# Projecting Q ahead of K, taking the recurrence's rows later, and summing three modulation pieces in place on DVE

## The chip, the cores and the metric

The kernel runs on one core of a Trainium2 chip. The time is that of one execution on the device, in microseconds (us); smaller is better. The kernel before took 792.27 us, the median of three runs (791.53 to 793.74).

The engines are named as in the profile: PE is TensorE's matmul, PEld its weight load, DVE is VectorE, ACT is ScalarE, POOL is GpSimd, and SP is SyncE, which here does nothing but issue loads and stores. Each engine works through its own instructions in the order in which the program lists them; an instruction waits for the others by semaphores.

## The reference

Two layers over 256 latent tokens and 256 context tokens of width 1024, all in float32. Cut to what matters:

```python
for layer in range(2):
    mod = silu(c) @ ada_w[layer] + ada_b[layer]            # 6 * 1024 values: shift, scale, gate, twice
    shift1, scale1, gate1, shift2, scale2, gate2 = split(mod, 6)
    h = rmsnorm(x, norm_mix[layer]) * (1 + scale1) + shift1
    if layer == 0:
        q, k, v, xb, gb = split(h @ w_in, ...)             # also k, v, xb of the context tokens
        attn = neighbourhood_attention(norm(q), norm(k), v, ...)   # 8 heads, context keys in the same softmax
        y = bidirectional_rglru(conv(xb), ...)             # gates, then a scan in each direction
        mix = concat(attn, gelu(gb) * y) @ w_out
    else:
        mix = real(fft2(h by groups of channels)) @ fnet_w
    x = x + gate1 * mix
    h2 = rmsnorm(x, norm_ffn[layer]) * (1 + scale2) + shift2
    x = x + gate2 * grouped_moe(h2)                        # router, top 2 of 16 experts, silu(h g) * (h u) @ d
```

`mod` is a product of one vector with a 1024 x 6144 matrix in each layer. The kernel cuts that matrix into 12 pieces of 512 columns for each layer, named (layer, j). Pieces (1, 7), (1, 8) and (1, 9), which the change is about, hold the second half of layer 1's second shift and all of its second scale but no gate; they are first used when layer 1's expert stage begins.

## The kernel before

**Weights.** All large weights stream through 16 buffers ("slots") of 128 x 2048 float32, 1 MiB each. `Stream` holds a list of items in a fixed order. SP issues the next item's load as soon as a slot is free, and never an item ahead of its turn; a slot is free once the last instruction that reads it is done. A modulation piece is two slots (four of the eight 128-row blocks in each), a projection of 512 columns is two, an expert is two for each of its gate (`g`), up (`u`) and down (`d`) matrices. The order in the front is written out in `ORDER`: "a" is the next modulation piece of the list `ADA`, Q, G and V are projections, B the attention bias, o and p the halves of the output projection. Then come four more pieces of layer 0 and two of layer 1 (`FILL0`), the experts of layer 0 in pairs (g, u, d, each four slots), layer 1's mixing weights `fw`, the three pieces of `GAP` and two more (`FILL1`), and the experts of layer 1.

**A modulation piece on PE** (`ada_te`, L324): 32 products in four column tiles, the columns of a piece against the silu of the conditioning vector; ACT copies the result out of PSUM (`gvr`, L337), PE transposes it (L339), and DVE adds the bias into `modc` (L350). `ada_step` does this in two steps for the projections' loops: the products in the first, the transposes in the second. `side(n)` runs n such steps.

**Projections.** A weight block is split into a high part (ACT, L371) and a remainder (L372, on POOL or DVE), and three matmuls replace one (`mm3`, L384 to L386). `gemm` (L580) runs the eight blocks of a projection and splits two blocks ahead; the strings `EK`, `EQ`, `EG`, `EV` choose the engine of each remainder, "g" for POOL and "v" for DVE. Before the projections of this section, xb has been projected.

**The order of layer 0's mixing.** PE's order is written by hand (`manual_schedule`); the order on the other engines is made by a planner, which goes by the program's order as a priority and by when it holds an instruction to be ready. PE's order before: K's eight blocks, each followed by `conv(2)` (the convolution, DVE), by a modulation step and from block 3 on by the first direction's gates (`gates[0]`, strings `W_K`); then Q with the steps of the first direction's recurrence (`scan[0]`, string `W_Q`); then the gate branch G with the rest of `scan[0]` and the head norm's transposes (`hk`); then V with `hq`, `gates[1]` and `scan[1]`. Each `head_norm` has one step of arithmetic (ACT squares, DVE sums and scales) and then one step with transposes for each 128 tokens. Both directions' gates live in two buffers R and I, which the pool holds once: the second direction's are written when the first direction's scan is through. In `scan`, ACT makes the exponential, tanh and square root, DVE the sums and products and the scan itself, POOL the products with I.

Then a loop of 20 steps (L849) runs attention: unit u is a head and half of the queries. A step computes scores for two units (PE), the softmax of the unit before (DVE bias, DVE maximum, ACT exponential, DVE scaling) and the transposes of earlier ones. Beside it, steps 0 to 5 run a modulation step each, steps 0 to 3 run `cat_rec` (the recurrence's rows times the gate on POOL, split on ACT and POOL), and steps 4 to 17 run one step each of the output projection (`project`), two more coming after the loop.

**Experts** (`moe`, L875; `up`, L1034; `down`, L1066): a pair's gate and up products, `act` on DVE, PE transposes, the down products, then ACT and DVE make `yH` and `yL`, which `scatter` adds into the result. The first pairs come right after the router; pair p's weights are items (g, u, d) of p.

**Between the layers** (L1193 on): `normed` adds the experts' result and normalizes (DVE, ACT). Meanwhile PE has, ahead of the DFT in its order, the products of the three `GAP` pieces (`ada_pe`, L1195), whose transposes come after the normalized input (`issue_after`). Then the DFT (L1211 on), the projection with `fw`, and layer 1's experts.

## Time and profile before

| | before |
|---|---|
| median of three runs | 792.27 us (791.53 to 793.74) |
| the profiled execution | 794.38 us, of which the profile's span is 792.6 |
| mean granted clock of TensorE in it | 0.957 |
| PE busy | 708.8 us (89% of the span) |
| DVE, ACT, POOL busy | 277.2, 241.6, 129.6 us |
| loaded and stored | 277.41 MB, mean 350 GB/s |

The profile is of one execution. Its times count from the first instruction. PE's busy time includes time in which matmuls overlap in the pipeline, so 89% does not mean that PE is at its limit for that share. Averages over the span say little here, since the stages have different limits; the sections below go by stage. "Granted clock" is the share of full speed at which TensorE was clocked, at one of two levels (1.2 and 2.4 GHz), averaged over a stretch.

### The profile page before, as it was taken

The numbers are of one execution on the slowest core, as the hardware profiler recorded it, in microseconds if no ns is written. First come the engines' busy times: TensorE is split into PE (matmuls) and PEld (weight loads), VectorE is DVE, ScalarE is ACT, GpSimd is POOL, SyncE is SP. The second block draws the span as 40 slices with busy tenths as digits, with TensorE's granted clock in tenths as the row PEclk, the third lists the DMA queues.
The fourth block names the chain that finished last, engine by engine and source line by source line (L and its number), as shares of the span: only waits on it lengthen the run. The fifth ranks groups of instructions, "written<-read, shape, count | busy, mean of one in ns | idle before, by whom it ended". The sixth has DMA issues, their size and how long they took to land. (4 is left out here: it accounts for less than half of the span.)

```text
span 792.6 us, 11546 instructions
## 1 busy us (share of the span) xinstructions
PE 708.8 (89%) x4707; PEld 388.6 (49%) x4707; DVE 277.2 (35%) x551; ACT 241.6 (30%) x432; POOL 129.6 (16%) x109
## 2 busy tenths in 40 slices
PE   3999979994997799799999997899699799999996
PEld 2677659563775633343444333667434343344334
DVE  3556388166654511111121104344511111121115
ACT  6233955963665310100110003254310110111001
POOL 1243271363321200000000001032201000000002
PEclk8899998996999899999999999899799999999998
DMA  8989756485656789999999999999299999999995
GB/s 275 356 329 385 311 222 264 167 304 228 265 196 253 296 358 421 416 405 421 421 420 423 418 421 422 420 420 351 112 374 422 417 411 421 421 420 420 423 399 170
DMA packets 53793, 277.41 MB, mean 350 GB/s; under 512 B 4898, under 2 KB 20832, under 8 KB 22496
## 3 DMA queue, kind: packets, MB, share of 16 engines
q1 hardware_dynamic: 53008, 275.95, 87.0%
q8 instruction: 41, 0.67, 0.3%
q10 hardware_dynamic: 720, 0.59, 0.2%
q14 instruction: 24, 0.20, 0.1%
HBM read 275.47 MB, written 1.05 MB: 349 GB/s over the span
## 5 line engine op out<-in xcount | busy, mean ns | idle before, releaser
L1042 PE MATMUL g<-slot,xg 128*64 128x512 f32 x512 | 116.2, 608 | 7.9 <-PEq L1145 7.9
L1079 PE MATMUL dn<-slot,aT 128*64 128x512 f32 (+1 forms) x544 | 114.1, 571 | 3.2 <-DVE aT L1063 3.2
L1042 PE MATMUL u<-slot,xg 128*64 128x512 f32 x512 | 113.0, 592 | 0.0
L372 POOL TENSOR_TENSOR wp<-slot,wp 128x512 fp32r<-128x512 f32 x50 | 68.8, 1385 | 161.6 <-ACT wp L371 161.5
L1042 PEld LDWEIGHTS g<-slot,xg 128*64 128x64 f32 x512 | 38.3, 140 | 81.7 <-issue 80.8
L1048 DVE TENSOR_TENSOR act<-act,u 128x512 f32<-128x512 f32 x16 | 11.0, 687 | 192.1 <-PE u L1042 192.1
L1042 PEld LDWEIGHTS u<-slot,xg 128*64 128x64 f32 x512 | 38.0, 137 | 72.2 <-issue 71.7
L1079 PEld LDWEIGHTS dn<-slot,aT 128*64 128x64 f32 x544 | 37.5, 137 | 68.5 <-issue 60.2
L331 PE MATMUL gv<-slot,sc 128*32 128x128 f32 x1536 | 58.2, 293 | 12.1 <-DMA slot<-in_ada_w_dram 7.7
L1081 ACT ACTIVATE yH<-dn,gcol 128x512 fp32r<-128x512 f32 (+1 forms) x34 | 22.5, 662 | 130.5 <-PE dn L1079 125.3
L997 ACT ACTIVATE xg<-xg,modc,a 128x256 f32<-128x256 f32 x32 | 18.0, 564 | 136.5 <-PE xg L988 136.5
L331 PEld LDWEIGHTS gv<-slot,sc 128*32 128x32 f32 x1536 | 47.8, 118 | 24.0 <-issue 13.0
L999 POOL TENSOR_TENSOR SG<-S,gates 128x512 f32<-128x512 f32 x8 | 8.4, 1044 | 310.5 <-PE st L1051 302.1
L1082 DVE SCALAR_TENSOR_TENSOR yL<-dn,gcol,yH 128x512 fp32r<-128x512 f32 (+1 forms) x34 | 24.4, 719 | 93.6 <-ACT yH L1081 85.4
L371 ACT ACTIVATE wp<-slot 128x512 fp32r<-128x512 f32 x72 | 44.3, 627 | 38.0 <-PE qp L386 11.6
L1047 ACT ACTIVATE act<-g 128x512 f32<-128x512 f32 x16 | 9.6, 597 | 121.4 <-PE g L1042 121.4
L988 PE MATMUL xg<-S,xh 128*128 128x256 f32 x128 | 28.4, 306 | 3.8 <-DVE S L976 2.6
L995 DVE TENSOR_SCALAR xg<-xg,a,modc 128x256 f32<-128x256 f32 x32 | 17.4, 543 | 29.4 <-ACT xg L997 29.4
L988 PE MATMUL xg<-S,xl 128*128 128x256 f32 x128 | 27.4, 298 | 0.0
L1019 PE MATMUL ya<-yH,ST 128*128 128x512 f32 x60 | 26.2, 437 | 0.5 <-ACT yH L1081 0.2
L988 PEld LDWEIGHTS xg<-S,xh 128*128 128x128 f32 x128 | 22.1, 209 | 5.5 <-issue 3.2
L1019 PE MATMUL ya<-yL,ST 128*128 128x512 f32 x60 | 23.9, 399 | 0.9 <-DVE yL L1082 0.9
(252 smaller groups left out, 1047.0 us busy)
## 6 DMA issues: line engine op xcount, KB each, us to landing
slot<-in_moe_g_dram SPq DMA_DIRECT2D x64, 1024.0 KB, 13.5
slot<-in_moe_u_dram SPq DMA_DIRECT2D x64, 1024.0 KB, 15.2
slot<-in_moe_d_dram SPq DMA_DIRECT2D x60, 1024.0 KB, 16.3
slot<-in_ada_w_dram SPq DMA_DIRECT2D x40, 1024.0 KB, 8.3
slot<-in_w_in_dram SPq DMA_DIRECT2D x8, 1024.0 KB, 7.2
slot<-in_ada_w_dram SPq DMA_DIRECT2D x12, 512.0 KB, 9.0
slot<-in_w_out_dram SPq DMA_DIRECT2D x4, 1024.0 KB, 6.3
slot<-in_fnet_w_dram SPq DMA_DIRECT2D x4, 1024.0 KB, 19.8
```

What stands on the lines that cost most here:

```text
L331: te.matmul(out=p[32 * q:32 * q + 32, 0:128], lhsT=sc32[:, k, :], rhs=W[:, k, c:c + 128], start=(k == 0), stop=(k == 7))
L371: ac.activation(dst_h, src, AF.Copy)
L372: eng.tensor_tensor(dst_l, src, dst_h.bitcast(F32), op=ALU.subtract)
L988: at_xg[0] = te.matmul(out=p[:, i * 256:(i + 1) * 256], lhsT=xx[:, tb, k * 128:(k + 1) * 128], rhs=S[:, tb * 256:(tb + 1) * 256], start=(n ...
L995: ve.tensor_scalar(xg[:, k], pv, a2[:, k:k + 1], b2[:, k:k + 1], op0=ALU.mult, op1=ALU.add)
L997: ac.activation(xg[:, k], pv, AF.Identity, scale=a2[:, k:k + 1], bias=b2[:, k:k + 1])
L1019: te.matmul(out=yacc[tb * 2 + h], lhsT=ST[:, tb * 128:(tb + 1) * 128], rhs=y[:, h * 512:(h + 1) * 512], start=(p == 0 and n == 0), stop=(n ...
L1042: te.matmul(out=q[half(i), :], lhsT=xg[:, k, half(i0 + i)], rhs=W[i][:, k], start=(k == 0), stop=(k == 7))
L1048: ve.tensor_tensor(act, act, gu[1], op=ALU.mult)
L1079: te.matmul(out=dn[half(i), :], lhsT=aT[:, fc * 128 + 64 * i:fc * 128 + 64 * i + 64], rhs=W[i][:, fc, c], start=(fc == 0), stop=(fc == 3))
L1081: ac.activation(yH[:, c], dn, AF.Copy, scale=gcol)
L1082: ve.scalar_tensor_tensor(yL[:, c], dn, gcol, yH[:, c].bitcast(F32), op0=ALU.mult, op1=ALU.subtract)
```

## The change

- In the front, Q's projection comes ahead of K's. `conv`, one channel block a step, and five of the modulation steps go beside Q; the first direction's gates and the first steps of its recurrence beside K; the rest of that recurrence and the arithmetic of Q's head norm beside G, where K's transposes come one a step after block 3; Q's transposes go to V's first blocks. The stream's order (`ORDER`) follows. The strings that give each remainder's engine change: all of Q's on POOL, three of K's eight on DVE; G's and V's stay.
- One modulation piece less is done ahead of V, so the loop of attention runs other pieces, and (1, 6) comes after the loop (`side(99)`).
- In the loop, `cat_rec` runs in steps 2 to 5 rather than 0 to 3, and the output projection in steps 6 to 19 rather than 4 to 17.
- Pieces (1, 7), (1, 8), (1, 9) are loaded after the down weights of layer 0's pairs 4, 5 and 6 rather than after `fw`. The new `ada_inplace` multiplies and adds a piece's eight blocks into its first one on DVE (8 instructions of 128 x 512) after the pair's down products; one pair later, after `up`, PE sums over the partitions with four products against a column of ones, and DVE adds the bias. The products in PE's order between the layers go.

```diff
--- before.py
+++ after.py
@@ -31,20 +31,21 @@
 
 FILL0 = [[(0, 10), (0, 11)], [(1, 4), (1, 5)], []]
 FILL1 = [[(1, 10), (1, 11)], [], []]
-GAP = [(1, j) for j in (7, 8, 9)]
-
-ORDER = 'aaaQaBaaGaaVaapoa'
-
-EK = 'ggggvggg'
-EQ = 'vgvgvgvg'
+
+BESIDE = [(1, j) for j in (7, 8, 9)]
+
+ORDER = 'aaKaaBaGaaVaaapoa'
+
+EK = 'gvggvggv'
+EQ = 'gggggggg'
 EG = 'vgvgvgvg'
 EV = 'ggvggvgg'
 EO = 'ggvggvggvggvggvg'
 EF = 'vvggggvggvvggvgg'
 
-W_K = ('11111111', '00022220')
-W_Q = ('00010000', '11311111')
-W_G = ('00010000', '12221100', '00001111')
+W_Q = '11101010'
+W_K = ('00100010', '22220000', '00001222')
+W_G = ('00010000', '22221000')
 W_V = ('01001010', '00001321', '22220000')
 
 
@@ -229,6 +230,8 @@
                 r += [(c, a // 512, slice(a % 512, a % 512 + b - a)) for a, b in zip(CUTS, CUTS[1:]) for c in pair]
             else:
                 r += [(c, i) for i in range(2) for c in pair]
+            if l == 0 and n == "d" and p - 4 in range(len(BESIDE)):
+                r.append(ada_item(*BESIDE[p - 4]))
         return r
 
     WQ, WK, WV, WXB, WGB = range(5)
@@ -280,7 +283,7 @@
         load_ada(ks)
         load_wx(ks[0])
 
-    st.add([win_item(WK)])
+    st.add([win_item(WQ)])
     st.pump()
 
     cols = const.tile([128, 190], F32, name="cols")
@@ -364,6 +367,23 @@
         second = ada_te(l, [(W, q * 128, 4 * j + q) for q in range(4)], ps_=wps, used=W.used, late=True)
         yield
         second()()
+        yield
+
+    def ada_inplace(l, j):
+
+        W = st.get(("a", l, j))
+        r = W[:, 0]
+        ve.tensor_scalar(r, r, sc32[:, 0, 0:1], None, op0=ALU.mult)
+        for k in range(1, 8):
+            ve.scalar_tensor_tensor(r, W[:, k], sc32[:, k, 0:1], r, op0=ALU.mult, op1=ALU.add)
+        W.done(1)
+        yield
+        p = wps("gv")
+        for q in range(4):
+            te.matmul(out=p[:, q:q + 1], lhsT=r[:, q * 128:(q + 1) * 128], rhs=ones[:, 0:1], start=True, stop=True)
+        c4 = slice(4 * j, 4 * j + 4)
+        ve.tensor_tensor(modc[l][:, c4], p[:, 0:4], ada_b[l][:, c4], op=ALU.add)
+        W.done(0)
         yield
 
     def split(dst_h, src, dst_l, eng):
@@ -534,7 +554,7 @@
     gw = [t[:, 1536:2048].rearrange("p (d b j) -> p d b j", d=2, b=4) for t in bg]
     for g in range(2):
         nc.sync.dma_start(out=gw[g], in_=gate_w[:, g])
-    named = {"Q": [win_item(WQ)], "G": [win_item(WGB)], "V": [win_item(WV)],
+    named = {"K": [win_item(WK)], "G": [win_item(WGB)], "V": [win_item(WV)],
              "B": [(bias_t[i], na_bias[:, 4 * i:4 * i + 4]) for i in range(2)],
              "o": [st.chunk(("wo", 1), w_out[1])], "p": [st.chunk(("wo", 0), w_out[0])]}
     ada = iter(ADA)
@@ -544,7 +564,7 @@
     st.add([ada_item(*a) for n in FILL0 for a in n])
     st.add(exp_items(0))
     st.add([st.chunk(("fw", h), fnet_w[h]) for h in range(2)])
-    st.add([ada_item(*a) for a in GAP + [a for n in FILL1 for a in n]])
+    st.add([ada_item(*a) for n in FILL1 for a in n])
     st.add(exp_items(1))
     for c in (a_s[1], a_s[3], Wx):
         for i in range(2):
@@ -677,47 +697,49 @@
 
     by_hand = ExitStack()
     by_hand.enter_context(tc.manual_schedule(engines={mybir.EngineType.PE}))
-    kp = [acc("kp") for _ in range(4)]
     conv = Task(convolution())
     rec = [Recurrence(d) for d in range(2)]
     gates = [Task(r.gates()) for r in rec]
     scan = [Task(r.scan()) for r in rec]
     side = Task(*[ada_step(*a) for a in ADA])
-    for n, _ in enumerate(gemm(st.get(("win", WK)), lambda w, k: rows(kp, w, 4, k), EK)):
-        conv(2)
-        side(int(W_K[0][n]))
-        if n == 3:
-            softplus()
-        gates[0](int(W_K[1][n]))
-    evacuate(kp, kr)
-    gates[0](99)
-    side(1)
     qp = [acc("qp") for _ in range(2)]
     for n, _ in enumerate(gemm(st.get(("win", WQ)), lambda w, k: rows(qp, w, 2, k), EQ)):
-        scan[0](int(W_Q[1][n]))
-        side(int(W_Q[0][n]))
+        conv(1)
+        side(int(W_Q[n]))
+        if n == 5:
+            softplus()
+    conv(99)
     qr = [t2k("qr")[:, 0:512] for _ in range(2)]
     evacuate(qp, qr)
+    side(1)
+    kp = [acc("kp") for _ in range(4)]
+    for n, _ in enumerate(gemm(st.get(("win", WK)), lambda w, k: rows(kp, w, 4, k), EK)):
+        gates[0](int(W_K[1][n]))
+        scan[0](int(W_K[2][n]))
+        side(int(W_K[0][n]))
+    evacuate(kp, kr)
     hk, hq = Task(head_norm(kr, kT, kn)), Task(head_norm(qr, qT, qn8))
     hk(1)
-    hq(1)
     side(1)
     gb2 = [acc("gbp") for _ in range(2)]
     gbp = [gb2[b // 2][:, (b % 2) * 256:(b % 2) * 256 + 256] for b in range(4)]
     for n, _ in enumerate(gemm(st.get(("win", WGB)), lambda w, k: channels(gbp, w, 256, k), EG)):
         scan[0](int(W_G[1][n]))
         side(int(W_G[0][n]))
-        hk(int(W_G[2][n]))
+        if n == 1:
+            hq(1)
+        if n > 3:
+            hk(1)
     scan[0](99)
+    hk(99)
     evacuate(gb2, [gTf[:, 0:512], gTf[:, 512:1024]])
-    hk(99)
     side(1)
 
     vp = [acc("vp") for _ in range(4)]
     for n, _ in enumerate(gemm(st.get(("win", WV)), lambda w, k: rows(vp, w, 4, k), EV)):
         side(int(W_V[0][n]))
-        if n == 0:
-            hq(99)
+        if n < 2:
+            hq(1)
         gates[1](int(W_V[2][n]))
         scan[1](int(W_V[1][n]))
         if n == 6:
@@ -725,6 +747,7 @@
         if n % 4 == 3:
             st.give(s_h[n // 4])
             st.give(s_h[2 + n // 4])
+    hq(99)
     scan[1](99)
     v = a8("v", [128, 4, 512])
     for t in range(4):
@@ -850,9 +873,9 @@
         att()
         if u < 6:
             side(1)
-        if u < 4:
+        if 2 <= u < 6:
             cat()
-        elif u < 18:
+        if u >= 6:
             mp = next(mix)
     side(99)
     att(99)
@@ -1099,6 +1122,8 @@
                     gate = gate_rows(l, 40)
                     overflow(l, ci, over, xh, xl, a2, b2, gate)
                 u = up(p, xg)
+                if l == 0 and p - 5 in range(len(BESIDE)):
+                    next(beside)
                 if p == 0:
                     for f in fins:
                         f()
@@ -1118,6 +1143,9 @@
                 if p == 5 and l == 0:
                     load_dft()
                 pend = down(u[0], act_t, *u[2:])
+                if l == 0 and p - 4 in range(len(BESIDE)):
+                    beside = ada_inplace(*BESIDE[p - 4])
+                    next(beside)
                 if p % 2 == 1 and p < 7:
                     xg = xg_
             if store:
@@ -1192,13 +1220,9 @@
     dts = []
     xn, _ = normed(mp, gate)
     yacc, gate = moe(0, xn, False)
-    fins = [ada_pe(*a, ps_=(gps, wps, wps)[i]) for i, a in enumerate(GAP)]
 
 
     xn, last = normed(yacc, gate, a8("xn", [128, 2, D]))
-    with tc.issue_after(last.ins):
-        for f in fins:
-            f()
     dt = dts[0]
     a1 = scale_col("a1_1", modc[1], 8, g_mix[1])
     b16 = const.tile([128, 8], F32, name="b16")
```

## Rows read from the trace of the kernel before

**Rows 1.** Stages: us, busy PE, PEld, DVE, ACT, POOL (x), clock, DMA, GB/s.
```profile
103.00:123.00 20.00, 14.84 (x61) 10.65 (x65) 19.09 (x22) 7.67 (x15) 11.21 (x8) 0.83 0.54 211
123.00:140.00 17.00, 17.00 (x238) 16.43 (x230) 12.43 (x20) 11.23 (x22) 4.48 (x4) 1.00 0.67 249
...
175.00:190.00 15.00, 4.11 (x76) 3.11 (x77) 11.56 (x20) 5.10 (x12) 8.17 (x10) 0.70 0.72 281
...
276.00:490.00 214.00, 204.69 (x977) 83.70 (x974) 37.22 (x65) 25.41 (x41) 6.92 (x5) 0.99 0.99 411
490.00:572.00 82.00, 63.32 (x558) 47.49 (x558) 40.50 (x92) 34.73 (x74) 18.72 (x13) 0.90 0.84 342
```

**Rows 2.** What SP's load queue waited for: us in total, times, longest us.
```profile
SPq L128 <- PE g L1042: 104.5, 22, 24.3
```

**Rows 3.** SP in order of time, 455 to 500: start, length, count.
```profile
456.04 8.04 SPq L128 DMA_DIRECT2D slot<-in_moe_d_dram  x4
...
476.21 22.68 SPq L128 DMA_DIRECT2D slot<-in_ada_w_dram  x10
```

**Rows 4.** The loads of 455 to 464.5, issue to landing.
```profile
DMA to landing us min/median/max: 20.1/20.1/20.1
```

**Rows 5.** PE in order of time, 380 to 585: start, us, [idle before <-releaser].
```profile
480.44 7.09 PE L1079 MATMUL dn<-slot,aT 128*64 128x512 f32 x32
...
496.15 1.94 PE L331 MATMUL gv<-slot,sc 128*32 128x128 f32 x32 [5.61 <-DMA slot<-in_ada_w_dram]
...
507.12 2.68 PE L1211 MATMUL f<-dft,xn 128*128 128x257 f32 x10
...
509.73 1.08 PE L331 MATMUL gv<-slot,sc 128*32 128x128 f32 x32
```

**Rows 6.** Groups by line, 276 to 490: count, busy us, mean ns.
```profile
L1082 DVE SCALAR_TENSOR_TENSOR yL<-dn,gcol,yH 128x512 fp32r<-128x512 f32 x16 | 12.0, 751 | 51.5 <-ACT yH L1081 47.4 <-issue 4.1
```

**Rows 7.** PE in order of time, 108 to 125, in Q.
```profile
111.76 0.51 PE L385 MATMUL qp<-wp,h 128*128 128x512 f32 x1 [0.89 <-POOL wp L372]
...
117.55 0.79 PE L385 MATMUL qp<-wp,h 128*128 128x512 f32 x1 [4.12 <-DVE wp L372]
...
118.14 0.63 PE L386 MATMUL qp<-wp,h 128*128 128x512 f32 x1
...
122.53 2.13 PE L331 MATMUL gv<-slot,sc 128*32 128x128 f32 x64
```

**Rows 8.** DVE in order of time, three stretches.
```profile
69.39 4.42 DVE L577 SCALAR_TENSOR_TENSOR xcT<-xb,cols,xcT 128x512 f32<-128x512 f32 x5
...
184.24 1.27 DVE L762 TENSOR_REDUCE mx<-s 128x1 f32<-128x512 f32 x2
...
498.91 0.75 DVE L417 TENSOR_SCALAR xn<-xt,rs 128x1024 f32<-128x1024 f32 x1
```

**Rows 9.** The table of stages, 496 to 503.
```profile
496.00:503.00 7.00, 5.60 (x97) 4.11 (x97) 2.85 (x6) 1.72 (x4) 0.00 (x0) 0.58 1.01 418
```

**Rows 10.** ACT in order of time, two stretches.
```profile
146.79 1.26 ACT L641 ACTIVATE R<-gp,cols 128x512 f32<-128x512 f32 x2
...
186.31 0.42 ACT L371 ACTIVATE catH<-yl 128x256 fp32r<-128x256 f32 x1 [1.63 <-POOL yl L737]
...
188.04 0.69 ACT L765 ACTIVATE P<-s,mx 128x512 f32<-128x512 f32 x1
```

**Rows 11.** PE in order of time, two stretches around attention.
```profile
189.04 0.47 PE L339 MATMUL gv<-cst,gvr 128*128 128x128 f32 x1 [10.19 <-ACT gvr L337]
...
198.77 1.50 PE L331 MATMUL gv<-slot,sc 128*32 128x128 f32 x46 [0.69 <-ACT PT L781]
...
242.65 0.41 PE L331 MATMUL gv<-slot,sc 128*32 128x128 f32 x2 [0.93 <-DVE catL L372]
```

**Rows 12.** POOL in order of time, 60 to 80.
```profile
70.59 2.67 POOL L372 TENSOR_TENSOR wp<-slot,wp 128x512 fp32r<-128x512 f32 x1 [5.84 <-ACT wp L371]
...
78.35 1.27 POOL L372 TENSOR_TENSOR wp<-slot,wp 128x512 fp32r<-128x512 f32 x1 [3.40 <-ACT wp L371]
```

## The prediction

> **What bounds the kernel now.** I read the table of stages first, then the load queue, then TensorE around each place that the diff touches.
>
> The stages [rows 1] show two kinds of time. In layer 0's expert stage (276 to 490 us) the DMA share is 0.99 at 411 GB/s, so the load stream sets the pace. Ahead of it, from 103 to 190 us, the DMA share is 0.54 to 0.72 and PE has holes. In the bridge between the two expert stages (490 to 572) DMA falls to 0.84.
>
> The load queue shows what ties the stages together. It waits for PE's gate products to free a buffer for 104.5 us in all, 24.3 at the longest [rows 2]: this is the bridge's end, with all 16 buffers full. So layer 1's experts always start with the same stock, and the end of the kernel is their start plus a constant. That start is layer 0's start, plus its expert stage, plus the bridge. I cost each of the three.
>
> Is layer 0's expert stage bound by PE or by DMA? By both at once. Its last four loads are issued from 456.04 to 464.08 [rows 3] and land 20.1 us after issue [rows 4], so the last at about 483.8. The last down product starts at 480.44 and takes 7.09 [rows 5]; its second half, which needs that load, starts at 484.0. There is no slack.
>
> **Part 1, three pieces move into the expert loads: +14.9.** Each piece is two buffers, so six more stand in the queue ahead of layer 0's last down weights. Ten such loads were issued in 22.68 us under a full queue [rows 3], (22.68 - 0.33)/9 = 2.48 us each. Six are 14.9, and with no slack the end of the stage moves by all of it. If PE's clock falls while it waits for loads, the last half-product (3.5 us) could take twice as long: bounds 14.9 to 18.4.
>
> The summing on DVE is 24 instructions of 128x512, bounded by yL's 0.75 us [rows 6]: at most 18 us. They hide, since DVE is busy for 37 of the 214 us [rows 1]. The added wait is for the piece's load; behind it on DVE stand the next pair's products, for which PE's transposes wait. But weights queued after a piece land after it, so PE stands for those anyway; without that cover one piece is up to 6 us. The 12 one-column products on PE, between zero and the 0.63 us of a slow 512-column one [rows 7] (7.6 in all), lie in PE's waits too.
>
> **Part 2, the bridge without those pieces: -5.7.** Now PE has the three pieces' products ahead of the DFT in its order and waits for their loads, at first 5.61 us [rows 5]. The normalized input is there at 498.91 + 0.75 = 499.7 [rows 8], the DFT starts at 507.12, and 1.08 us of a piece still lies inside it [rows 5]. Without them it can start 7.5 earlier and run 1.1 shorter: -8.6. What is late next is that input, off DVE. But PE then does nothing from 490 to 499.7, and the DFT meets the lower clock. After the shorter idle time of now, 496 to 503 has a granted clock of 0.58 [rows 9], so 7 us x 0.42 = 2.9 are lost. Bounds: nothing, and twice that, as the idle time is nearly twice as long. I take 2.9, the row of the same place.
>
> **Part 3, the front: -5.0.** Removed: the Q projection stops twice, 0.89 and 4.12 us, for weight splits, the longer time on DVE; then 11 matmuls from 117.55 to 122.53 run at the lower clock (0.63 us each) [rows 7], which loses half of 5 us. Together 7.5. The recurrence's arithmetic fills DVE at that time: 19.09 of 20 us busy [rows 1]. In the new order it comes with K's end and with G. One piece (two halves of 1.08 [rows 5], 2.1 us) also leaves the part ahead of V. If nothing came in their place, V would start 9.6 earlier.
>
> What comes in their place? The recurrence now meets K's head norm on DVE, beside G, and four of G's eight splits are on DVE. The two windows from 103 to 140 hold 31.5 us of DVE work [rows 1], which the new order packs from K's last steps into G, so DVE is as full as in the stretch that stalled. The return is between 0 and 7.5; I take 3.75, half: the arithmetic is the same, but K's steps, twice Q's in length, can take some of it. Separately, V's gates need the buffers that the first direction holds until DVE is done: 31.5 us from about 105 end at about 137, against a need at 146.79 [rows 10] less 9.6. That just fits. So V gains 5.85, and with it the second direction's scan.
>
> Attention starts late now: PE stands 10.19 us until 189.04 [rows 11], behind ACT, which writes the last output row at 186.31 and loads a table before the first exponential at 188.04 [rows 10]. The first of the two row maxima that end at 184.24 + 1.27 [rows 8] is there at 184.9. With those output rows two units later, the exponential could come 3.1 earlier. But ACT's order is a planner's, and these rows already run there ahead of exponentials that the program issues first; so 0 to 3.1, and I take 1.5.
>
> The piece that left the front comes back after attention: 2.1, plus up to 0.47 for its transposes, less the wait of 0.93 that it covers [rows 11]: +1.6. The output projection moves from units 4 and 5 to 18 and 19, so these two have less to hide the softmax. Such a unit waits 0.69 now [rows 11]: 0 to 1.4, I take 0.7. The front is -5.85 - 1.5 + 1.6 + 0.7 = -5.0.
>
> The loads that change places in the front cost nothing as long as PE's freeing of buffers sets their times; the idle DMA there [rows 1] is the cover. Without it, one load is 2.5.
>
> One more effect can touch Q. POOL now makes all eight split remainders while DVE runs the convolution; a split takes 1.27 us on POOL by itself and up to 2.67 [rows 12] beside that convolution (69.39 to 73.81 [rows 8]). Q's work on PE is 48 matmuls of 0.23 (half of the slow 0.45 in [rows 7]) and three pieces: 17.3 us. The Trainium skill ("SBUF — State Buffer", Who interferes with whom) says that a DVE instruction with two SBUF inputs and a GpSimd one that reads SBUF exclude each other for a whole instruction, and that speaks against this edit. The trace agrees with it in those two rows. By the rows alone: eight at 2.67 are 21.4, so 4.1 lost; with half at 1.27 they are 15.8, and nothing is lost. The convolution ends at 74, ahead of the last splits, so I count nothing here and keep 4.1 as a rival.
>
> **Sum.** +14.9 - 5.7 - 5.0 = +4.2 us. The profiled execution took 794.38, its span 792.6 and 1.8 around it; with the sum it is 798.6. It lies 2.1 over the median of 792.27, so the forecast is 796.5, 0.5% slower. A measurement can tell about 0.3% (2.4 us) from no change.
>
> **Rivals.**
> - *DVE keeps up in G* (the other side: not slower). Place: DVE between K's last steps and V. It decides whether splits and norms come in time, with the first direction's last scan before V's gates need its buffers. For it: K's longer steps. Against: the full DVE [rows 1]. Price: V gains 9.6, attention 3.1, no extra softmax wait: front -9.6 - 3.1 + 1.6 = -11.1, total -1.9, 790.4.
> - *The same, and the DFT meets the full clock*: a further -2.9, 787.5.
> - *The whole stop returns in G, and ACT's order stays*: front -2.1 + 1.6 + 0.7 = +0.2, total +9.4, 801.7. For it: the same instructions on the same engines.
> - *POOL is late in Q*: 796.5 + 4.1 = 800.6.
> - *The added loads cost nothing*, because the stream has room I don't see: 796.5 - 14.9 = 781.6. Against: [rows 1, 3].
> - *The later rows change nothing*, as ACT's order stays: 798.0, inside the forecast's own range of 793.5 to 799.5.
>
> **How the numbers follow.** Forecast 0.44 (0.34 of it slower by over 2.4 us, 0.10 within), DVE keeps up 0.24 (0.16 within, 0.08 faster), the full clock too 0.10 (faster), the stop returns 0.12, POOL late 0.05, loads free 0.05. Faster 0.08 + 0.10 + 0.05 = 0.23; within 0.10 + 0.16 = 0.26; slower 0.34 + 0.12 + 0.05 = 0.51. The range runs from 787.5, the full-clock case, to 801.7, the returning stop, and leaves out the free loads and half of each outer case's spread.
>
> **What would show it.** Part 1: PE waits for gate, up and down loads in the last three pairs of layer 0, some 15 us in all; no such waits, and it falls. Part 2: DFT within 1 us of the normalized input, clock near 0.6 at first. Part 3: no stop over 1 us in Q; in G, matmuls that wait for DVE's splits or for head norm; PE's stop at attention's start shorter than 10. I am wrong if the first expert stage grows by less than 12, or if V starts over 8 us earlier.

## The result and the profile after

| | before | after |
|---|---|---|
| median of the runs beside each other | 793.0 us | 800.24 us |
| profiled execution, its span | 794.38, 792.6 | 800.24, 798.2 |
| mean granted clock | 0.957 | 0.964 |

The ratio is 1.0084, with a 95% interval from 1.0066 to 1.0102: slower by 7.2 us, where 4.2 was forecast. The trace shows 5.6 of it (the spans). In stages, each worked out from the first or last start or end of the matmuls named, in us from the start:

| stretch | before | after | change | forecast |
|---|---|---|---|---|
| first projection matmul to layer 0's first gate matmul | 61.94 to 275.28: 213.3 | 61.47 to 275.09: 213.6 | +0.3 | -5.0 |
| layer 0's experts, to the end of the last down product | 487.52: 212.2 | 502.51: 227.4 | +15.2 | +14.9 |
| bridge, to layer 1's first gate matmul | 571.65: 84.1 | 577.63: 75.1 | -9.0 | -5.7 |
| layer 1's experts, to PE's last matmul | 215.3 | 215.4 | +0.1 | 0 |

(The first projection matmul itself came 0.5 earlier, and what follows PE's last matmul is 0.5 shorter.) So the largest term came as forecast, the front gave nothing of its 5.0, the bridge gave 3.3 more, and two errors partly cancel.

**Layer 0's experts.** After, PE's timeline from 440 to 503 (start, us, operation; in brackets the idle time before and what ended it) shows what [rows 5] did not have, waits for gate and up loads:

```profile
447.54 3.65 PE L1065 MATMUL u<-slot,xg 128*64 128x512 f32 x16 [0.77 <-DMA slot<-in_moe_u_dram]
452.51 3.65 PE L1065 MATMUL u<-slot,xg 128*64 128x512 f32 x14 [1.32 <-DMA slot<-in_moe_u_dram]
...
470.87 1.97 PE L1065 MATMUL g<-slot,xg 128*64 128x512 f32 x2 [4.04 <-DMA slot<-in_moe_g_dram]
473.35 8.64 PE L1065 MATMUL g<-slot,xg 128*64 128x512 f32 x29 [0.51 <-DMA slot<-in_moe_g_dram]
483.29 3.65 PE L1065 MATMUL u<-slot,xg 128*64 128x512 f32 x16 [0.86 <-DMA slot<-in_moe_u_dram]
488.27 3.65 PE L1065 MATMUL u<-slot,xg 128*64 128x512 f32 x14 [1.33 <-DMA slot<-in_moe_u_dram]
```

The waits named are 8.8 us of the 15.2. The rest lies inside groups that PE stretches while their weights arrive, such as the 8.64. On DVE, one piece's sums are 8 instructions, 0.49 + 2.32 + 3.11 = 5.9 us, and one of them waits:

```profile
465.66 0.49 DVE L376 TENSOR_SCALAR slot<-slot,sc 128x512 f32<-128x512 f32 x1 [0.67 <-DMA slot<-in_ada_w_dram]
468.29 2.32 DVE L378 SCALAR_TENSOR_TENSOR slot<-slot,sc 128x512 f32<-128x512 f32 x3
470.64 3.11 DVE L378 SCALAR_TENSOR_TENSOR slot<-slot,sc,slot 128x512 f32<-128x512 f32 x4
```

**The bridge.** The normalized input is there 12.1 us after the last down product in both kernels (before: [rows 5, 8]). After, on PE and on DVE:

```profile
511.70 9.26 PE L1235 MATMUL f<-dft,xn 128*128 128x257 f32 x32 [6.18 <-DVE xn L437]
520.81 0.59 PE L1252 MATMUL pq<-Y,dft 128*128 128x254 f32 x2
```
```profile
510.82 0.74 DVE L437 TENSOR_SCALAR xn<-xt,rs 128x1024 f32<-128x1024 f32 x1
...
513.90 0.75 DVE L437 TENSOR_SCALAR xn<-xt,rs 128x1024 f32<-128x1024 f32 x1
```

and the table of stages (us, busy time and count of PE, PEld, DVE, ACT, POOL, then clock, DMA share, GB/s):

```profile
511.70:514.60 2.90, 2.90 (x6) 1.82 (x6) 1.92 (x4) 1.45 (x3) 0.00 (x0) 0.50 1.01 415
514.70:520.80 6.10, 6.09 (x26) 5.06 (x27) 3.38 (x14) 2.47 (x7) 0.00 (x0) 0.98 1.01 422
```

The DFT does meet the lower clock: 0.50 of full speed, the level of 1.2 GHz. But it begins with the first 128 tokens, whose half of the input is there at 511.56, and only six of its 32 matmuls run on that half alone. They have nothing to hurry for: the second half comes at 514.65, and the seventh starts at 514.71. From there on the clock is 0.98.

**The front.** PE in G, after:

```profile
116.01 0.39 PE L406 MATMUL gbp<-h,wp 128*128 128x256 f32 x1 [1.74 <-DVE wp L392]
119.93 0.38 PE L406 MATMUL gbp<-h,wp 128*128 128x256 f32 x1 [0.80 <-DVE wp L392]
128.77 0.65 PE L637 MATMUL ht<-cst,kq 128*128 128x128 f32 x4 [4.44 <-DVE kq L631]
137.06 1.95 PE L334 MATMUL gv<-slot,sc 128*32 128x128 f32 x64 [0.53 <-DVE modc L353]
```
```profile
128.77:133.00 4.23, 4.23 (x23) 4.23 (x24) 4.23 (x4) 1.32 (x2) 2.89 (x3) 0.60 0.71 250
```

Q has no stop any more (PE is busy for 19.00 of the 19 us from 61 to 80), and G has 1.74 + 0.80 + 4.44 + 0.53 = 7.5 us of them, all for DVE, which is busy for 26.96 of the 27 us from 112 to 139. Behind the longest of them the clock is 0.60 for 4.2 us (the second block: stretch, busy times, clock), which loses 1.7 more: 9.2 in all, where Q lost 5.0 by stops and 2.5 by the clock [rows 7]. At attention's start, first DVE, then ACT, then PE:

```profile
183.18 1.27 DVE L785 TENSOR_REDUCE mx<-s 128x1 f32<-128x512 f32 x2
```
```profile
185.26 0.42 ACT L391 ACTIVATE catH<-yl 128x256 fp32r<-128x256 f32 x1 [1.63 <-POOL yl L760]
185.69 1.28 ACT L788 ACT_TABLE_LOAD   x1
186.99 0.69 ACT L788 ACTIVATE P<-s,mx 128x512 f32<-128x512 f32 x1
...
187.66 0.27 ACT L340 ACTIVATE gvr<-gv 128x128 f32<-128x128 f32 x1
```
```profile
187.98 0.47 PE L342 MATMUL gv<-cst,gvr 128*128 128x128 f32 x1 [11.10 <-ACT gvr L340]
```

The four output rows (catH) still stand ahead of the first exponential (P), though the program now issues them later; PE's stop is 11.10, against 10.19 [rows 11].

The +0.3 of the whole front is in part luck. Up to the end of the output projection it is 1.2 longer (187.3 against 186.1, from the first projection matmul). The stretch behind that, the same code in both, gives 0.9 back, and there the clock differs. Here are its last matmuls, which gather the experts' tokens, before and after:

```profile
269.82:275.25 5.43, 5.43 (x32) 5.33 (x32) 1.30 (x3) 1.69 (x3) 0.97 (x1) 0.69 0.85 353
```
```profile
271.11:275.20 4.09, 4.09 (x34) 3.96 (x36) 1.45 (x3) 1.70 (x3) 0.97 (x1) 1.00 1.01 427
```

### The profile page after: what moved, and what is told of

Its sections match the earlier page's. It is cut to its first block, busy times and chain, and to the rows that moved or that the text cites. A ratio compares the mean times of both kernels' runs of the same rounds, so it can differ in the third digit from the quotient of the medians.

```text
span 798.2 us, 11217 instructions
## 1 busy us (share of the span) xinstructions
PE 708.3 (89%) x4536; PEld 385.6 (48%) x4536; DVE 295.5 (37%) x573; ACT 245.3 (31%) x432; POOL 133.8 (17%) x111
## 5 line engine op out<-in xcount | busy, mean ns | idle before, releaser
L1065 PE MATMUL g<-slot,xg 128*64 128x512 f32 x512 | 119.4, 611 | 13.6 <-PEq L1173 7.8
L1065 PE MATMUL u<-slot,xg 128*64 128x512 f32 x512 | 115.6, 593 | 4.3 <-DMA slot<-in_moe_u_dram 4.3
L392 POOL TENSOR_TENSOR wp<-slot,wp 128x512 fp32r<-128x512 f32 x52 | 73.6, 1422 | 152.2 <-ACT wp L391 152.1
L334 PE MATMUL gv<-slot,sc 128*32 128x128 f32 x1344 | 50.4, 288 | 3.8 <-ACT sc L307 2.0
L334 PEld LDWEIGHTS gv<-slot,sc 128*32 128x32 f32 x1344 | 41.2, 115 | 14.1 <-issue 7.2
L392 DVE TENSOR_TENSOR wp<-slot,wp 128x512 fp32r<-128x512 f32 x20 | 17.9, 898 | 19.7 <-ACT wp L391 19.7
## 6 DMA issues: line engine op xcount, KB each, us to landing
slot<-in_moe_d_dram SPq DMA_DIRECT2D x60, 1024.0 KB, 16.2
slot<-in_w_in_dram SPq DMA_DIRECT2D x8, 1024.0 KB, 12.1
```

Source lines behind the costliest of these rows:

```text
L334: te.matmul(out=p[32 * q:32 * q + 32, 0:128], lhsT=sc32[:, k, :], rhs=W[:, k, c:c + 128], start=(k == 0), stop=(k == 7))
L392: eng.tensor_tensor(dst_l, src, dst_h.bitcast(F32), op=ALU.subtract)
L1065: te.matmul(out=q[half(i), :], lhsT=xg[:, k, half(i0 + i)], rhs=W[i][:, k], start=(k == 0), stop=(k == 7))
```

## The experiments

A short table first; the sections behind it say what each is. V start, row maximum (end of attention's first two) and first P transposes count from the first projection matmul; all of them and the three stages are worked out from each kernel's trace, the ratio from its runs.

| kernel | median us | ratio, 95% interval | V start | row max. | P transposes | first gate matmul | layer 0 | bridge |
|---|---|---|---|---|---|---|---|---|
| before | 793.0 | | 78.0 | 123.6 | 133.1 | 213.3 | 212.2 | 84.1 |
| after | 800.2 | 1.0084 [1.0066, 1.0102] | 77.5 | 123.0 | 132.8 | 213.6 | 227.4 | 75.1 |
| e2_beside | 800.2 | 1.0076 [1.0052, 1.0100] | 78.3 | 123.9 | 133.6 | 213.8 | 227.7 | 75.5 |
| e5_pe_beside | 799.0 | 1.0069 [1.0052, 1.0086] | 77.0 | 122.6 | 132.1 | 212.4 | 227.2 | 75.4 |
| e3_swap | 784.0 | 0.9886 [0.9856, 0.9915] | 77.1 | 122.6 | 132.1 | 212.4 | 212.1 | 74.4 |
| e4_without | 783.4 | 0.9873 [0.9853, 0.9893] | 77.6 | 123.2 | 132.5 | 212.7 | 212.1 | 74.5 |
| e1_front | 797.1 | 1.0044 [1.0023, 1.0065] | 77.2 | 122.8 | 132.6 | 215.8 | 212.6 | 88.4 |
| e8_rows_early | 797.2 | 1.0048 [1.0031, 1.0065] | 77.8 | 123.3 | 133.1 | 214.0 | 212.3 | 84.0 |
| e10_g_pool | 796.8 | 1.0051 [1.0036, 1.0066] | 77.8 | 123.6 | 133.4 | 214.2 | 212.3 | 83.9 |
| e7_kt_in_v | 797.7 | 1.0045 [1.0027, 1.0062] | 69.9 | 123.0 | 132.1 | 215.4 | 212.8 | 85.0 |
| e6_front_order | 792.4 | 0.9978 [0.9959, 0.9996] | 77.2 | 122.7 | 128.8 | 210.1 | 212.3 | 84.8 |
| e9_swap_order | 783.4 | 0.9862 [0.9824, 0.9899] | 77.7 | 123.3 | 130.1 | 211.1 | 212.7 | 75.4 |
| e11_modc_act | 784.0 | 0.9882 [0.9858, 0.9906] | 78.0 | 123.6 | 130.6 | 210.2 | 212.3 | 77.1 |
| e12_sum_pool | 783.5 | 0.9897 [0.9856, 0.9937] | 78.0 | 122.2 | 128.2 | 207.0 | 212.1 | 77.1 |

How far these numbers can be trusted is seen in the rows that share their front's code: before, e2, e3, e4 and e5 give 77.0 to 78.3 for V's start and 212.4 to 213.8 for the first gate matmul. Each trace is of one execution, and need not agree with the median: those of e1, e2 and e11 are of the longest run of their kernel, those of e3, e5, e8 and e12 of the shortest.

### The pieces: loads or sums?

`e2_beside` is the pieces' part of the change on the front of before. `e5_pe_beside` also has the loads there, but multiplies on PE:

```diff
                 pend = down(u[0], act_t, *u[2:])
                 if l == 0 and p - 4 in range(len(BESIDE)):
-                    beside = ada_inplace(*BESIDE[p - 4])
-                    next(beside)
+                    ada_pe(*BESIDE[p - 4], ps_=wps)()
```

> The pieces' part of the change alone, on the front of the kernel before. Theory (six loads more in a stream that is the bound of layer 0's experts cost 15; the bridge without the pieces' products gives 9): stage of layer 0 +15, bridge -9, 799 us, and with the front's -0.2 this is the whole change. Rival (the front and the pieces' part are not independent: a later or earlier start of the experts changes what the added loads cost): more than 2 us off 799.

> The three pieces loaded beside layer 0's last experts as in the change, on the front of the kernel before, but multiplied on PE there (64 products of 32x128 each, about 2 us a piece), not summed on DVE. Theory (the cost of this part is the six loads in a full stream; what consumes them is hidden in PE's waits for those loads): layer 0's stage again 15 longer, within 2 us of the run with the sums on DVE, 799 to 802 us. Rival (the sums on DVE, with their waits ahead of the next pair's products, are a good part of those 15): 3 us or more below the run with the sums, 797 or less.

Both theories held: 227.7 and 227.2 for layer 0, whatever consumes the pieces. With PE's products the same waits stand in PE's timeline:

```profile
471.70 3.65 PE L1044 MATMUL g<-slot,xg 128*64 128x512 f32 x16 [1.36 <-DMA slot<-in_moe_g_dram]
...
481.64 3.65 PE L1044 MATMUL u<-slot,xg 128*64 128x512 f32 x16 [1.32 <-DMA slot<-in_moe_u_dram]
```

The cost is the six loads in a full stream, and DVE's sums spare PE nothing that it would have missed.

### The pieces: what was late in the bridge?

`e3_swap` is before with one change in the order of loads; `e4_without` is before without the three pieces.

```diff
-    st.add([st.chunk(("fw", h), fnet_w[h]) for h in range(2)])
-    st.add([ada_item(*a) for a in GAP + [a for n in FILL1 for a in n]])
+    st.add([ada_item(*a) for a in GAP])
+    st.add([st.chunk(("fw", h), fnet_w[h]) for h in range(2)])
+    st.add([ada_item(*a) for n in FILL1 for a in n])
```

> The kernel before with one change: the three pieces' loads stand ahead of the four loads of the output projection's weights (fw) instead of behind them, still behind layer 0's last down weights; products on PE as before. Theory (the pieces are late in the bridge only because their loads land late, 5.6 us first and under 1 us four times after): stage of layer 0 unchanged; four loads of 2.48 us earlier, so the products fall into PE's idle time from 490.5 to 499.7; the DFT starts near 500 instead of 507.1; total -8 to -9, 784 to 785 us. Rival (the output projection then waits for its own weights, or layer 1's experts find a smaller stock): -3 or less, 790 us or more.

> The kernel before without the three pieces: neither their loads nor their products; the twelve columns that they give are the bias alone, so layer 1's experts see other shifts, scales and gates. It is the lower bound of what can be had from moving these pieces. Theory (with the loads swapped, all three lie in PE's idle time and cost nothing): within 2 us of the swapped run (784.0), bridge 74 to 75 us, layer 0's stage 212. Rival (they still cost their loads, 6 x 2.48 us, somewhere in the stream, up to layer 1's experts): 5 us or more below the swapped run, 779 or less.

Held. In e3_swap, from the last down product (it ends at 485.46) on:

```profile
486.06 0.62 PE L331 MATMUL gv<-slot,sc 128*32 128x128 f32 x10
...
494.77 1.08 PE L331 MATMUL gv<-slot,sc 128*32 128x128 f32 x32
...
495.78 2.68 PE L1212 MATMUL f<-dft,xn 128*128 128x257 f32 x10
```
```profile
486.00:496.00 10.00, 7.96 (x170) 5.80 (x170) 7.42 (x15) 4.99 (x11) 0.00 (x0) 1.00 1.01 420
496.00:503.00 7.00, 7.00 (x59) 5.39 (x59) 3.17 (x14) 3.39 (x9) 0.00 (x0) 1.00 1.01 419
```

The products, which waited 5.61 us for their loads before [rows 5], now fill PE's idle time. The DFT starts 10.3 us after the last down product instead of 19.6, PE's clock ahead of it stays at 1.00 where it was 0.58 [rows 9], and the bridge is 74.4. Leaving the pieces out gives 74.5 and the same time within the intervals: in this place they cost nothing that can be measured. So the whole gain of the bridge is to be had without the 15 us; e3_swap beats both kernels.

### The front alone

> The front part of the change alone; the three pieces stay where they were, loaded behind the first experts and multiplied ahead of the DFT. Theory (the stops of the Q projection only move to the G projection, and attention waits for the same DVE and ACT work): layer 0's experts start within 1 us of the kernel before (275.3), total -0.2, 793 us. Rival, the sum on record: -5.0, 788 us, experts start at 270. Rival that the front itself costs time which the rest gives back: +2 us or more, 795.

> The front part alone, with the recurrence's output rows and the output projection's steps put back to their earlier units. Theory (ACT's order puts these rows ahead of the exponentials in either case, so the later place gives nothing): within 1 us of the front alone, 796 to 798 us; PE's stop at the start of attention again 10 to 11. Rival, the record's 1.5 for the stop less 0.7 for the last units: 0.8 slower; or the opposite, the moved steps cost up to 2 us in the first units: 795 us.

```diff
-        if 2 <= u < 6:
+        if u < 4:
             cat()
-        if u >= 6:
+        elif u < 18:
             mp = next(mix)
```

The front alone is 3.5 us slower in the median; the last of the rivals has the sign, but no reason for it. Its trace has 2.4 more up to the first gate matmul: 1.2 up to the projection's end, as in after, and 1.2 behind it, where the gather has a clock of 0.59 (271.3 to 278.1). It has 4.3 more in the bridge, whose code is that of before: the DFT starts 1.7 later and takes 1.8 longer, at a clock of 0.80 (511.6 to 522) against 1.00 before (507.1 to 515.8). The traces of e8 and e10 have a bridge of 84 with the same median, and there the front costs 0.6 and 0.9. But e1's trace is of a run of 801.45, the longest of seven, and theirs are of 795.09 and 795.19, 2.15 and 1.62 under their medians, so whether their other runs have the longer bridge too isn't known. What makes the 3.5 stays open. On top of the pieces no cost of the front can be told: 800.2 with it (after) and without it (e2).

With the rows early the median is the same, and the stop at attention again 11.10: the later rows give nothing, as the theory had it. From the first P transposes to the projection's end e8 takes 53.7, e1 54.7, so the two late units do cost about 1.0 in the traces, which the medians don't show.

`e10_g_pool` puts all of G's split remainders on POOL; `e7_kt_in_v` moves K's transposes from G into V (there G's result is written over two of K's four row tiles ahead of their transposes, so the attention works on other keys).

```diff
-EG = 'vgvgvgvg'
+EG = 'gggggggg'
```
```diff
-        if n > 3:
-            hk(1)
     scan[0](99)
-    hk(99)
...
-        if n < 2:
-            hq(1)
+        if n < 6:
+            (hk if n < 4 else hq)(1)
```

> The front part alone, with all eight weight splits' remainders of the G projection on POOL, where four were on DVE. Theory (PE's three stops in G come from too much work on DVE there, the recurrence and K's head norm; four splits of 0.69 to 1.76 us less): the two stops behind splits, 1.74 and 0.80, fall by half or more, the one behind head norm (4.4) to 3 or less; V starts 2 to 4 us earlier; attention's first row maximum moves by less than 1, so the time stays within 1.5 of the front alone (797.1). Rival (POOL, slower at a split, becomes the one that is late): the stops in G stay or grow.

> The front part alone, with the four transposes of K's head norm moved from the G projection into the first steps of V, so that PE meets no stop of 4.4 us for DVE in G. Theory (V's earlier start is worth little, since the second direction's recurrence fills ACT from 144 to 167 us and DVE from 167 to 183, and the first exponential follows that): V starts about 4 us earlier, attention's first row maximum less than 2 us earlier, 795 to 797 us against 797.1 for the front alone. Rival, the step on record (V's gain carries through to attention in full): 4 us, 793 us.

e10's theory of G failed. PE's timeline in G:

```profile
117.46 0.58 PE L387 MATMUL gbp<-h,wp 128*128 128x256 f32 x1 [2.42 <-POOL wp L373]
122.80 0.38 PE L387 MATMUL gbp<-h,wp 128*128 128x256 f32 x1 [0.92 <-POOL wp L373]
130.42 0.91 PE L618 MATMUL ht<-cst,kq 128*128 128x128 f32 x4 [2.91 <-DVE kq L612]
```

The stops behind splits now name POOL and are longer; only head norm's fell, 4.42 to 2.91, and V starts no earlier: the three stops are 6.25 in all, but the clock is 0.87 from 114.5 to 140, where e1 has 0.94 from 112.5 to 139.3. DVE is still busy for 23.86 and POOL now for 21.27 of these 25.5 us. The row maximum and the time stayed within what was expected.

In e7 V's start is not what counts. V starts 7.3 earlier than in e1, and attention's row maximum 0.3 later:

```profile
137.90 0.80 PE L385 MATMUL vp<-wp,h 128*128 128x512 f32 x1 [4.06 <-DVE kq L595]
```
```profile
183.33 1.27 DVE L763 TENSOR_REDUCE mx<-s 128x1 f32<-128x512 f32 x2
```
```profile
144.00:167.00 23.00, 23.00 (x163) 15.27 (x162) 3.19 (x7) 21.50 (x30) 7.95 (x6) 1.00 0.37 134
167.00:183.20 16.20, 9.85 (x105) 7.65 (x103) 16.17 (x20) 8.99 (x14) 8.85 (x7) 0.92 0.86 353
```

Four of the 7.3 go at once to a wait for DVE's copy of G's result. The rest goes to ACT (21.50 of 23 us busy; the transposes' evictions are now in V too, but after has 22.05 in the same window without them) and to DVE behind it (16.17 of 16.2), on the second direction's recurrence.

### Attention's start

`e6_front_order` is e1 with ACT's order written out.

```diff
-            split(catH[:, 4 + b], yv[:, b], catL[:, 4 + b], gp)
+            with tc.issue_after(exps[1].ins):
+                split(catH[:, 4 + b], yv[:, b], catL[:, 4 + b], gp)
...
-        ac.activation(P, s, AF.Exp, bias=mx, accum_out=sm)
+        with tc.issue_after(copies[-1].ins):
+            exps.append(ac.activation(P, s, AF.Exp, bias=mx, accum_out=sm))
```

> The front part alone, and ACT's order at the start of attention written out: the piece's copy (gvr) ahead of the first exponentials, and the four output rows of the recurrence (catH) behind the first two exponentials. Theory (PE's stop of 11.1 us is ACT's order: PE waits for gvr at 187.98 while 6 us of products and scores stand ready behind it, and the first exponential waits 2.5 to 3 us behind catH rows): the stop falls below 5, the first exponential comes at about 184.5, layer 0's experts start 3 to 7 us earlier, 786 to 790 us. Rival (the softmax's work on DVE and ACT sets the pace of the whole loop, so the time returns as waits later in it): 792 to 794 us.

792.4 lies in the rival's range, but both ranges were reckoned from a front at 793, and the front alone turned out at 797.1. Against that, ACT's order is worth 4.7 us, and in the trace the first gate matmul comes 5.6 earlier, 4.3 of it by the projection's end and 1.3 by the clock behind it: the theory's 3 to 7. ACT, then PE:

```profile
184.23 0.69 ACT L773 ACTIVATE P<-s,mx 128x512 f32<-128x512 f32 x1 [5.37 <-DVE mx L769]
...
185.57 1.33 ACT L374 ACTIVATE catH<-yl 128x256 fp32r<-128x256 f32 x4
```
```profile
184.92 2.21 PE L760 MATMUL s<-kq 64*128 64x256 f32 x8 [6.97 <-DVE modc L353]
```

The first exponential came when expected, 184.2, but PE's stop did not fall below 5: the next scores wait for a sum of 0.15 us (modc) in DVE's queue. `e11_modc_act` gives that sum to ACT, on top of `e9_swap_order`, which is before with the swapped loads, this ACT order and the later rows. `e12_sum_pool` then takes four 128x256 sums from DVE's recurrence.

```diff
-                    ve.tensor_tensor(yv[:, cb], yv[:, cb], h[:, 0:256], op=ALU.add)
+                    gp.tensor_tensor(yv[:, cb], yv[:, cb], h[:, 0:256], op=ALU.add)
```

> The kernel before with its own front, the three pieces' loads ahead of the output projection's weights, and ACT's order at the start of attention written out (the piece's copy ahead of the first exponentials, the recurrence's rows behind the first two, these rows and the projection's steps two units later). Theory (both gains stand in different stages and add: -9.7 and -4.7): 779 to 780 us. Rival (a start of the experts that comes earlier finds their loads later, so one of the gains is given back): 783 or more.

> As the run with the swapped loads and ACT's order written out, and the first piece's four sums with its bias at the start of attention go on ACT instead of DVE, so that PE's next scores don't wait for a DVE that is full with the recurrence. Theory (PE's stop of 6 to 7 us there is now that one sum, 0.15 us long, in DVE's queue behind the second direction's recurrence; 4.9 us of scores and products stand behind it): the stop before the second scores goes, the first transposes of P come 4 to 5 us earlier (191.2 to about 186.5), 778 to 780 us. Rival (the softmax chain of the following units on DVE and ACT takes the time back): first transposes earlier, but the projection's end less than 2 earlier, 782 us or more.

> As the run before, and the four sums of the two directions' rows (128x256) go on POOL instead of DVE. Theory (the solid stretch of DVE work, the second direction's recurrence, ends last ahead of the first row maximum): the first row maximum comes 1.4 earlier, since two of these take 0.73 us on DVE, and the time falls by about as much, 777 to 779. Rival (something else ends last there, or POOL's sums hold DVE up): no earlier row maximum, same time or slower.

In e9 the two gains did not add: 783.4, the rival's time, where 779 to 780 was expected. In e11 two of the eight scores come ahead of the stop, which then only gets another name; the first P transposes come no earlier (130.6, against 130.1 in e9). So the theory fails, and 784.0 is the rival's time but not by its reason, which had the transposes earlier. In e12 the row maximum comes 1.4 earlier and the transposes 2.4. PE of e11, PE of e12, DVE of e12:

```profile
186.18 2.07 PE L764 MATMUL s<-kq 64*128 64x256 f32 x6 [4.70 <-ACT P L777]
```
```profile
183.87 2.05 PE L764 MATMUL s<-kq 64*128 64x256 f32 x6 [3.31 <-ACT P L777]
```
```profile
182.32 1.27 DVE L773 TENSOR_REDUCE mx<-s 128x1 f32<-128x512 f32 x2
```

So the chain that sets attention's start is DVE's recurrence, row maximum, exponential; scores come behind it. But the gain does not reach the medians: e9, e11 and e12 stand at 783.4 to 784.0 like e3, though e12's front is 5.4 shorter in the trace. Its bridge is 2.7 longer than e3's, and 1.4 of that is the DFT, at a clock of 0.83 (490.7 to 501) where e3 has 1.00; e11's bridge is the same. In e9's trace the front is 2.7 shorter up to the projection's end, and 1.3 of that goes by the clock in the gather. e12's four runs lie 7 us apart (779.75 to 786.90). Whether an earlier start brings such losses, or they fall as they fall, is not settled.

## Why the forecast was right in sign and near in size

**Part 1 (+14.9) held**: 15.2. Six loads at 2.48 each, with no slack, is the whole account, and e5 excludes the sums. The sign named for it, 15 us of PE waits for loads, shows as 8.8 of waits and the rest as stretched groups.

**Part 2 (-5.7) was too small**, by the term of the clock. The forecast took 2.9 off for the DFT at the lower clock. The clock was as forecast, but the step assumed that the whole DFT follows the whole input. It begins on half the tokens and waits for the rest, so the slow matmuls lie in a wait and cost nothing. Without the term the sum is -8.6, against -10.0 from the last down product to the first product behind the DFT (28.26 to 18.30); the other 1.4 is what the DFT does ahead of the second half. About 1 us is given back up to layer 1's first gate matmul.

**Part 3 (-5.0) failed**, at three steps.
- *The return of Q's stop.* It was put between 0 and 7.5, and half was taken. More than the upper bound came back: V started 0.5 earlier, where it would have been 9.6 with nothing in the stop's place, so 9.1, about the 7.5 of stops and 1.7 of clock above. "K's steps, twice Q's in length, can take some of it" is the step that failed. They took almost nothing, since what the recurrence has for DVE waits there for ACT; DVE beside K, and the table of stages for that stretch:

```profile
91.24 1.28 DVE L676 SCALAR_TENSOR_TENSOR lt<-A,R 128x512 f32<-128x512 f32 x1 [7.63 <-ACT R L670]
98.02 1.77 DVE L676 SCALAR_TENSOR_TENSOR lt<-A,R 128x512 f32<-128x512 f32 x1 [5.50 <-ACT R L670]
...
107.73 0.69 DVE L681 SCALAR_TENSOR_TENSOR A<-A,R 128x512 f32<-128x512 f32 x1 [6.46 <-ACT R L678]
```
```profile
83.61:107.73 24.12, 24.12 (x158) 15.60 (x157) 3.74 (x5) 23.11 (x30) 7.64 (x6) 1.00 0.73 290
```

  In these 24.12 us DVE worked for 3.74, and ACT for 23.11. From the first projection matmul to V's start ACT also loads a table 11 times, where it was 8 before, at 1.28 each. So nearly all of the recurrence meets G. No run took work from ACT beside K, so this is read from the waits. In G some of DVE's time is slow, too. Its splits there, and POOL:

```profile
114.20 1.76 DVE L392 TENSOR_TENSOR wp<-slot,wp 128x512 fp32r<-128x512 f32 x1
...
118.17 1.70 DVE L392 TENSOR_TENSOR wp<-slot,wp 128x512 fp32r<-128x512 f32 x1
...
121.22 0.68 DVE L392 TENSOR_TENSOR wp<-slot,wp 128x512 fp32r<-128x512 f32 x1
```
```profile
113.96 1.44 POOL L683 TENSOR_TENSOR I<-I,A 128x512 f32<-128x512 f32 x1 [3.93 <-PE gv L334]
...
117.79 1.53 POOL L683 TENSOR_TENSOR I<-I,A 128x512 f32<-128x512 f32 x1 [0.69 <-DVE A L681]
...
122.73 1.29 POOL L392 TENSOR_TENSOR wp<-slot,wp 128x512 fp32r<-128x512 f32 x1 [1.72 <-ACT wp L391]
```

  The same split takes 1.76 and 1.70 while POOL works, and 0.68 while it is idle; PE's first two stops end with the two slow ones. The Trainium skill ("SBUF — State Buffer", Who interferes with whom) says "A DVE instruction with two SBUF inputs contends with a GpSimd instruction that reads SBUF"; the rows agree. The forecast had looked for this in Q, as the rival of a late POOL, and not in G; in Q no stop came. It is not new, though: Q's long stop before ended with such a split, of 1.68.
- *"V gains, and with it the second direction's scan."* That step was not examined, and e7 speaks against it.
- *Attention's stop (-1.5).* Of the bounds 0 and 3.1 it was 0: the planner kept the order, as the text feared. The price was right, though: with the order enforced (e6) the first exponential comes 3.2 earlier than in e1, and the median is 4.7 lower. On the front of before with the swapped loads (e9, against e3) it comes 2.5 earlier, and the median is the same.

The returning piece and the softmax together were put at 2.3; from the first P transposes to the projection's end after has 1.5 more (53.05 to 54.58).

**The rival** "the whole stop returns, and ACT's order stays" comes nearest to the front: +0.2 forecast, +0.3 in the trace. That the two agree so well is luck: V gained 0.5 and not its 2.1, and 0.9 came from the clock ahead of the experts, for which it has no term. It had a chance of 0.12; its total, 801.7, is 1.5 off the 800.2 measured, the forecast's 796.5 is 3.7 off, and both hold the 2.9 of clock that wasn't lost.

## What to carry to other kernels

Before work is moved to another engine, ask whether its data could only have come earlier: here three lines of load order gave all that the pieces' move could give, without its price. Before an idle engine is counted on to take work earlier, ask what that work waits for: beside K DVE had the time, but its inputs came from ACT, which had none. In a stage where every engine in the chain is full, a stop that goes from one matmul group comes back in the next; look for the chain (here recurrence, row maximum, exponential), and cost the step that it ends on. And count a slow clock only where the work that meets it ends last.

## What the runs showed of the hardware

The 34 matmuls of the gather ahead of layer 0's experts come after the same stop in all kernels (1.66 to 1.67 us), yet the clock granted to them differs. In the three with the full clock (after, e10 and e12) the stop ahead of that one is 1.35 to 1.36 us, in the others 1.79 to 1.81. Here are e9 and e12, whose gather is the same code:

```profile
265.50:272.30 6.80, 6.77 (x34) 6.66 (x36) 1.63 (x3) 1.69 (x3) 1.00 (x1) 0.55 0.67 281
```
```profile
264.40:268.45 4.05, 4.05 (x34) 3.92 (x36) 1.40 (x3) 1.70 (x3) 0.97 (x1) 1.00 1.02 427
```

At 0.55, nearly all at the level of 1.2 GHz, they take 6.8 us; at 1.00 they take 4.05. The Trainium skill ("TensorE: Matmul & The Clock Gate", Part 1: The HAM clock gate) says that the moment of the change depends on where the first matmul falls against a watch that runs on by itself, and varies by 500 ns; the rows lie further apart than that, and none shows the cause. One such place gives or takes up to 2.7 us, which is about what separates several of the kernels here, and it need not be the doing of the edit.
